# Stationary weights read with a step of two words: two blocks of 128 columns interleaved in memory, in an fp32 encoder on one core

## The chip, the core and the metric

One NeuronCore of a Trainium2 chip runs the whole kernel in one launch. The metric is device time in microseconds, the median of three timed runs. The engines are named as the profile names them: PE (TensorE, matmuls), PEld (TensorE's weight loads, which overlap PE), DVE (VectorE), ACT (ScalarE), POOL (GpSimd) and SP (SyncE, which issues the weight transfers). A matmul has a *stationary* operand, which a weight load (LDWEIGHTS) puts into the array first, and a *moving* operand, which is streamed through it column by column.

## The reference, cut to what matters

Two encoder layers over 272 tokens (16 meta tokens and 256) of width 2048, everything in float32. Layer 0 mixes tokens by a Fourier transform, layer 1 by a bidirectional state-space mixer (SSD); each is followed by a SwiGLU block of hidden width 5632.

```python
def fourier_mixer(u, w_out):
    ug = u.astype(jnp.float32).reshape(b, L, FNET_GROUPS, d // FNET_GROUPS)
    f = jnp.fft.fftn(ug, axes=(1, 3), norm="ortho").real.reshape(b, L, d)
    return f.astype(u.dtype) @ w_out
...
def bidir_ssd_mixer(u, w_in, conv_w, conv_b, dt_bias, a_log, d_skip, norm_w, w_out):
    proj = u @ w_in
...
    return gated_group_rms_norm(y, z, norm_w) @ w_out

def swiglu_ffn(u, w_gate, w_up, w_down):
    return (jax.nn.silu(u @ w_gate) * (u @ w_up)) @ w_down
```

The time goes into the products with the weight matrices: `fnet_w_out`, `ssd_w_in`, `ssd_w_out`, and two each of `ffn_w_gate`, `ffn_w_up` and `ffn_w_down`.

## The kernel before

The residual stands feature-major: 16 blocks of 128 features on the partitions, 272 (later 256) tokens along the free dimension. To keep float32 accuracy every product is made of three matmuls on operands of type float32r. `mm3` (lines 104 to 106) multiplies high part by high part, high by low and low by high; each of the three loads its stationary operand anew.

A weight matrix comes in units of 1 MiB. The host lays each matrix out in blocks (`blocks`), so that a partition's 1024 consecutive words (`RUN`) are four rows of 256 columns or two rows of 512 columns. `weights` (line 84) issues one transfer per unit on SP's queue and splits the unit in two (or more) tiles: ACT writes the high part `wh` (line 97), DVE the low part `wl` (line 98).

In most products the weights are stationary and the tokens move. `wsl` (line 108) cuts the stationary operand out of a split tile: row block k, and 128 neighbouring columns from `c0`. That is 128 consecutive words of each partition, 512 bytes. Two blocks of columns, j = 0 and 1, are worked on in turn and go to two PSUM tiles. The users are `gemm_in` (the products with `ffn_w_gate`, `ffn_w_up` and the x, B, C columns of `ssd_w_in`; moving operand `gh`, `gl`), the product with `fnet_w_out` (moving `fh`, `fl`), `down0` (the first `ffn_w_down`; moving `hh`, `hl`), `out_group` (`ssd_w_out`; moving `yh`, `yl`) and the step sizes (`w_dt`, one block of 128 columns). The moving operand is 272, 258 or 256 tokens wide.

In two products the tokens are stationary and 512 columns of weights move: the z columns of `ssd_w_in` (stationary `gh`, `gl`) and the second `ffn_w_down` in `down1` (stationary `hh`, `hl`).

The order of the work is that of the program text, but for the splits, which are given a higher priority, and the rest of the SSD mixer, which is emitted at a distance behind the large products (`later`, `slot_done`). That rest holds plain float32 matmuls (lines 605 to 665) and transposes (lines 551 to 553; 794 in the last SwiGLU).

Of the kernel before, what the change touches and what calls it, by code (L numbers as in the profile page):

```python
# [12 lines left out]
F32R = mybir.dt.float32r  # L13
# [8 lines left out]
NB = D // P            # 16 feature blocks  # L22
NM = 16                # meta tokens
KM = 64 + NM           # rows that hold them three times, from 0, 32 and 64
S = 256
L = NM + S             # 272
FG = 8                 # fnet groups
FD = D // FG           # 256
NK = L // 2 + 1        # 137 token frequencies
# [4 lines left out]
HG = H // G            # heads per group  # L34
NST = 128
DFF = 5632
NF = DFF // P          # 44
EPS = 1e-6
CA = (NM, NM + P)      # token chunk A
CB = (NM + P, L)       # token chunk B  # L40
XC, BC, CC = 0, DI, DI + G * NST      # columns of x, B, C
NRAW, NSP = 3, 4       # buffers: weights as they come (8 KiB a partition), their parts (4 + 4 KiB)
RUN = 1024             # words of a weight block that a partition holds one after the other
HC = 8                 # feature blocks of a piece of the SwiGLU hidden layer
# [4 lines left out]
def encoder(ctx: ExitStack, tc: tile.TileContext, I, out):  # L49
# [34 lines left out]
    def weights(src, k0, nk, c0, ncol):  # L84
        """Unit of a weight matrix (see blocks), rows (k0..k0+nk)*128, columns c0..c0+ncol, as (high, low) parts."""
        w = wpool.tile([P, nk, ncol], F32, tag="w", name="w", bufs=NRAW)
        k1 = RUN // ncol
        nc.sync.dma_start(w.rearrange("p (u k) c -> p u (k c)", k=k1),
                          src[k0 // k1 : (k0 + nk) // k1, c0 // ncol].rearrange("u p x -> p u x"))
        parts = []  # L90
        n = min(nk, RUN // ncol)
        for k in range(0, nk, n):
            ks = slice(k, k + n)
            wh = wpool.tile([P, n, ncol], F32R, tag="wh", name="wh", bufs=NSP)
            wl = wpool.tile([P, n, ncol], F32R, tag="wl", name="wl", bufs=NSP)
            with tc.high_priority(offset=70):
                SC.copy(wh, w[:, ks, :])  # L97
                V.tensor_tensor(out=wl, in0=w[:, ks, :], in1=wh.bitcast(F32), op=ALU.subtract)  # L98
            parts.append((wh, wl))
        return parts  # L100

    def mm3(ps, lhs, rhs, start, stop):
        """ps (+)= lhs.T @ rhs of operands split as (high, low)."""
        PE.matmul(ps, lhs[0], rhs[0], start=start, stop=False)  # L104
        PE.matmul(ps, lhs[0], rhs[1], start=False, stop=False)  # L105
        PE.matmul(ps, lhs[1], rhs[0], start=False, stop=stop)  # L106
# [4 lines left out]

    def gsl(k, a, b=L):
        return gh[:, k, a:b], gl[:, k, a:b]

    def gemm_in(src, c0, lo):
        """Two blocks of 128 columns of norm(h) @ src, feature-major, over the tokens lo.. ."""
        n = L - lo
        pss = [mmtile(), mmtile()]
        for k0 in (0, 8):
            u = weights(src, k0, 8, c0, 256)  # L120
            for k in range(8):
                for j in range(2):
                    mm3(pss[j][:, :n], wsl(u, k, j * P), gsl(k0 + k, lo), k0 + k == 0, k0 + k == NB - 1)
        return pss

    def rsqrt(pool, x, n, tag):
        """1/sqrt(x) of [P, n]: bit-level seed and three Newton steps."""
# [14 lines left out]
    def norm_block(b, wcol, lo):  # L142
        """Block b of the residual is final: operand of the next product and sum of squares."""
# [10 lines left out]
    def norm_scale(lo):  # L154
        """rbc = 1/rms of every token, the same on all partitions."""
# [19 lines left out]
    # =====================================================================  # L175
    # Fourier mixer
    # =====================================================================
    with ExitStack() as fx:
# [15 lines left out]
        # parts of x where the spectrum comes later  # L194
# [49 lines left out]
        def table(c, r):  # L244
            """Token table of chunk c scaled by 1/rms."""
            SC.activation(th[:, c, :], tok[:, c, :], AF.Identity, bias=0.0, scale=r)
            V.scalar_tensor_tensor(out=tl[:, c, :], in0=tok[:, c, :], scalar=r, in1=th[:, c, :].bitcast(F32),
                                   op0=ALU.mult, op1=ALU.subtract)

        with tc.manual_schedule():  # L250
            # residual, feature-major, parts of x, mean squares of the tokens
# [37 lines left out]
            # meta tokens: three products of parts in one, rows 0.. high high, 32.. high low, 64.. low high  # L289
# [8 lines left out]
            # token transform: cosines 0..NK-1, sines 1..NK-2  # L298
# [20 lines left out]
        # feature transform; operands in F32R have an even number of columns, so one more than is used  # L319
# [24 lines left out]
        for mp in range(NB // 2):  # L344
            pss = [mmtile(), mmtile()]
            for k0 in (0, 8):
                u = weights(I["fnet_w_out"], k0, 8, mp * 256, 256)
                for k in range(8):
                    for j in range(2):
                        mm3(pss[j][:, :L], wsl(u, k, j * P), (fh[:, k0 + k, :], fl[:, k0 + k, :]),  # L350
                            k0 + k == 0, k0 + k == NB - 1)
# [5 lines left out]
    # =====================================================================  # L357
    # SwiGLU, the hidden layer in pieces of HC feature blocks
    # =====================================================================
# [32 lines left out]
    with ExitStack() as fx:  # L392
        tmp = fx.enter_context(tc.tile_pool(name="ffn0", bufs=1))

        def down0(f0, nf, hh, hl):
            for mp in range(NB // 2):
                pss = [mmtile(), mmtile()]
                u = weights(I["w_down0"], f0, nf, mp * 256, 256)
                for k in range(nf):
                    for j in range(2):  # L400
                        mm3(pss[j][:, :L], wsl(u, k, j * P), (hh[:, k, :], hl[:, k, :]), k == 0, k == nf - 1)
# [8 lines left out]
    # =====================================================================  # L410
    # bidirectional SSD mixer
    # =====================================================================
    with ExitStack() as fx:
# [22 lines left out]
        # The products with the large weights are emitted in slots; the rest of a group follows its slots at a  # L436
        # distance, so that the tensor engine has a product to go on with meanwhile.
# [12 lines left out]
        def step_sizes():  # L450
# [6 lines left out]
            # 1/rms of the tokens of chunks A and B, one token a partition  # L457
# [14 lines left out]
            # softplus(v) = max(v, 0) + log1p(exp(-|v|)), log1p(t) = 2 atanh(t / (2 + t))  # L472
# [16 lines left out]
            # prefix sums within the chunks: inclusive forward, exclusive backward  # L489
# [42 lines left out]
        def conv(ps, blk, lo, dst):  # L532
            """Depthwise conv over the tokens lo.. of the 128 channels of block blk, then silu."""
# [14 lines left out]
        def to_tokens(src, dst, dstM):  # L548
            """[128 channels, 272 tokens] -> [tokens, 128 channels] of the chunks A, B and of the meta tokens."""
# [7 lines left out]
        def out_group(gi, q, yh, yl):  # L557
            """Residual += y @ w_out over the channels of group gi, columns 512q.. ."""
            u = weights(w_out, gi * 4, 4, q * 512, 512)
            for jp in range(2):  # L560
                pss = [mmtile(), mmtile()]
                for k in range(4):
                    for j in range(2):
                        mm3(pss[j][:, :S], wsl(u, k, (2 * jp + j) * P), (yh[:, k, :], yl[:, k, :]), k == 0, k == 3)
# [6 lines left out]
        def group_rest(gi, cT, btok, btokM, xt, xtM, zs, cb):  # L571
            """All of a group after its products with w_in."""
# [5 lines left out]
            def kernels(c):  # L578
                """Within chunk c: sum over both directions of exp(decay) dt B.C, [source, head, target]."""
# [11 lines left out]
            # weighted inputs  # L591
# [27 lines left out]
            def mix(c):  # L619
                """y of chunk c: other chunks' parts, this chunk's part, skip connection; then the gate."""  # L620
# [31 lines left out]
            def norm():  # L652
                """Grouped norm, back to feature-major."""
# [32 lines left out]
        def decays(gi):  # L686
            """Cumulated log decays of a group's heads on all partitions."""
# [7 lines left out]
        def drop(gi):  # L695
            """The half that a direction doesn't see decays to nothing."""
# [11 lines left out]
        for gi in range(G):  # L708
            if gi % 2 == 0:
# [14 lines left out]
            # x of the group  # L724
# [4 lines left out]
            def source_target(gj=gi % 2, cb=cb, bT=bT, cT=cT):  # L729
                """B.C of all sources and targets within the chunks."""  # L730
# [16 lines left out]
            # silu(z) of the group  # L747
# [27 lines left out]
    # =====================================================================  # L775
    # last SwiGLU, final norm
    # =====================================================================
    with ExitStack() as fx:
# [8 lines left out]
        def down1(f0, nf, hh, hl):  # L787
            if f0 == 0:
                # residual, one token a partition
# [59 lines left out]
def tables():  # L849
    """Constants that follow from the shapes."""  # L850
# [19 lines left out]

def blocks(w, ncol):
    """[.., rows, columns] in blocks [rows of blocks, columns of blocks, 128, (k c)]: RUN words, that is RUN / ncol
    rows 128 apart of ncol columns, one after the other."""
# [6 lines left out]
def arrays_of(inputs):  # L880
    """The matrices in blocks, the per-feature vectors one after the other in rows of 128, the tables."""
# [3 lines left out]
    a["fnet_w_out"] = blocks(inputs["fnet_w_out"][0], 256)  # L885
    a["w_z"] = blocks(w[:, :DI], 512)
    a["w_xbc"] = blocks(w[:, DI : -2 * H], 256)
    a["w_dt"] = blocks(w[:, -2 * H :], P)
    a["ssd_w_out"] = blocks(inputs["ssd_w_out"][0], 512)
    a["ffn_w_gate"] = blocks(inputs["ffn_w_gate"], 256)  # L890
    a["ffn_w_up"] = blocks(inputs["ffn_w_up"], 256)
    a["w_down0"] = blocks(inputs["ffn_w_down"][0], 256)
# [17 lines left out]
```

## Time and profile before

| what | us |
|---|---|
| timed runs, median (lowest to highest) of 3 | 2456.85 (2456.33 to 2457.35) |
| profiled execution, from first to last instruction (span) | 2455.8 |
| PE busy in it | 2428.0 (99%) |
| PEld busy | 2316.9 (94%) |
| DVE busy | 1484.5 (60%) |
| ACT busy | 1214.1 (49%) |
| POOL busy | 406.6 (17%) |

How to read it: a matmul in a stream is shown from its start until its results have drained, so consecutive matmuls overlap in the table of instructions; what one costs is the distance from its start to the start of the next. The same holds for weight loads. The span of the profiled execution lies 1.05 us under the median of the timed runs; that is what lies around the span.

### The profile page before, as it was taken

What the parts mean: (1) busy time and instruction counts of PE and PEld (TensorE: products, weight loads), DVE (VectorE), ACT (ScalarE), POOL (GpSimd) and SP (SyncE); (2) the same over time, 40 slices, a digit from 0 to 9 for tenths busy, and PEclk for the clock granted to TensorE, in tenths of its full rate; (3) what the DMA queues carried; (4) which work ended last, traced back from release to release, by engine and by line L of the source; (5) the groups of instructions that cost most, each with busy time, mean ns of one, the idle gap of its engine ahead of it and who ended that gap; (6) DMA issues with size and microseconds to landing.
All of it is one profiled execution on the core that took longest, in us unless ns stands there. A gap on an engine that the chain in (4) does not pass through costs nothing.

```text
span 2455.8 us, 42928 instructions
## 1 busy us (share of the span) xinstructions
PE 2428.0 (99%) x17958; PEld 2316.9 (94%) x17958; DVE 1484.5 (60%) x2020; ACT 1214.1 (49%) x1784; POOL 406.6 (17%) x361
## 2 busy tenths in 40 slices
PE   8999999999999999999999999999999999999998
PEld 8999999999999999888989989989999998989887
DVE  7564545545454568778668668668554555555556
ACT  6444333343434346878557558445444343444434
POOL 3111111010101112232221221112211010102000
PEclk9999999999999999999999999999999999999999
DMA  5555555555555555655455555454555555555553
GB/s 164 175 178 179 173 173 176 181 175 172 175 181 177 172 173 175 213 175 186 164 179 193 177 172 184 159 172 157 201 187 178 189 189 189 189 190 188 189 192 134
DMA packets 115506, 438.66 MB, mean 179 GB/s; under 512 B 7360, under 2 KB 8080, under 8 KB 115136
## 3 DMA queue, kind: packets, MB, share of 16 engines
q1 hardware_dynamic: 110336, 417.86, 50.4%
q0 software_dynamic: 4832, 17.99, 2.3%
q8 instruction: 141, 2.31, 0.4%
q14 instruction: 53, 0.43, 0.0%
q10 hardware_dynamic: 144, 0.07, 0.0%
HBM read 433.66 MB, written 2.23 MB: 177 GB/s over the span
## 4 chain that ended last, share of the span: by engine, by line
PE 89%; DVE 3%; DMA 3%; issue 2%; ACT 2%; POOL 1%; SPq 0%; DVEq 0%; ACTq 0%; POOLq 0%
PE mm L105 29%; PE mm L106 28%; PE mm L104 28%; DMA pb<-scr 2%; DVE wl L98 1%; PE tp L642 1%; ACT wh L97 1%; DVE ca L544 1%; PE tp L626 0%; PE tp L665 0%; DMA w<-fnet_w_out 0%; POOL pb L701 0%; ACT pb L584 0%; DMA x<-x 0%; PE tp L608 0%
## 5 line engine op out<-in xcount | busy, mean ns | idle before, releaser
L98 DVE TENSOR_TENSOR wl<-w,wh 128x1024 fp32r<-128x1024 f32 x786 | 970.0, 1236 | 840.7 <-ACT wh L97 832.7
L97 ACT CAST wh<-w 128x1024 fp32r<-128x1024 f32 x786 | 822.8, 1048 | 1096.6 <-PE mm L105 809.2
L105 PE MATMUL mm<-gl,wh 128*128 128x272 f32 (+2 forms) x3600 | 1026.0, 285 | 0.0
L106 PE MATMUL mm<-gh,wl 128*128 128x272 f32 (+2 forms) x3600 | 1022.3, 284 | 0.5 <-DVE wl L98 0.5
L104 PE MATMUL mm<-gh,wh 128*128 128x272 f32 (+2 forms) x3600 | 1022.4, 284 | 0.1
L104 PEld LDWEIGHTS mm<-gh,wh 128*128 128x128 f32 x3600 | 678.2, 188 | 1.1 <-issue 0.5
L106 PEld LDWEIGHTS mm<-gh,wl 128*128 128x128 f32 x3600 | 676.3, 188 | 0.9 <-DVE wl L98 0.7
L105 PEld LDWEIGHTS mm<-gl,wh 128*128 128x128 f32 x3600 | 676.1, 188 | 0.8 <-issue 0.5
L378 POOL TENSOR_TENSOR s<-s,rbc 128x272 f32<-128x272 f32 (+1 forms) x88 | 96.4, 1113 | 816.4 <-ACT s L377 816.4
L105 PE MATMUL mm<-hl,wh 128*128 128x272 f32 x704 | 203.7, 289 | 0.0
L106 PE MATMUL mm<-hh,wl 128*128 128x272 f32 x704 | 202.7, 288 | 0.0
L104 PE MATMUL mm<-hh,wh 128*128 128x272 f32 x704 | 200.9, 285 | 0.0
L385 POOL TENSOR_TENSOR hl<-t,hh 128x272 fp32r<-128x272 f32 (+1 forms) x88 | 97.0, 1121 | 397.1 <-ACT hh L384 397.1
L104 PE MATMUL mm<-yh,wh 128*128 128x256 f32 x512 | 146.5, 288 | 3.8 <-DVE hT L567 3.3
L105 PE MATMUL mm<-yl,wh 128*128 128x256 f32 x512 | 143.6, 281 | 0.5 <-DVE yl L671 0.5
L106 PE MATMUL mm<-yh,wl 128*128 128x256 f32 x512 | 143.5, 281 | 0.0
L105 PE MATMUL mm<-wl,hh 128*128 128x512 f32 x352 | 137.1, 390 | 0.0
L104 PE MATMUL mm<-wh,hh 128*128 128x512 f32 x352 | 137.0, 389 | 0.0
L106 PE MATMUL mm<-wh,hl 128*128 128x512 f32 x352 | 137.0, 389 | 0.0
L104 PEld LDWEIGHTS mm<-hh,wh 128*128 128x128 f32 x704 | 132.9, 189 | 0.0
L106 PEld LDWEIGHTS mm<-hh,wl 128*128 128x128 f32 x704 | 132.3, 188 | 0.0
L105 PEld LDWEIGHTS mm<-hl,wh 128*128 128x128 f32 x704 | 132.1, 188 | 0.0
(279 smaller groups left out, 2858.5 us busy)
## 6 DMA issues: line engine op xcount, KB each, us to landing
w<-ffn_w_gate SPq DMA_DIRECT2D x88, 1024.0 KB, 5.1
w<-ffn_w_up SPq DMA_DIRECT2D x88, 1024.0 KB, 5.1
w<-w_down SPq DMA_DIRECT2D x80, 1024.0 KB, 5.1
w<-w_xbc SPq DMA_DIRECT2D x48, 1024.0 KB, 5.2
w<-w_z SPq DMA_DIRECT2D x32, 1024.0 KB, 5.3
w<-ssd_w_out SPq DMA_DIRECT2D x32, 1024.0 KB, 5.1
w<-fnet_w_out SPq DMA_DIRECT2D x16, 1024.0 KB, 5.1
pb<-scr POOLq DMA_DIRECT2D x32, 512.0 KB, 5.6
```

The source lines that it names most:

```text
L97: SC.copy(wh, w[:, ks, :])
L98: V.tensor_tensor(out=wl, in0=w[:, ks, :], in1=wh.bitcast(F32), op=ALU.subtract)
L104: PE.matmul(ps, lhs[0], rhs[0], start=start, stop=False)
L105: PE.matmul(ps, lhs[0], rhs[1], start=False, stop=False)
L106: PE.matmul(ps, lhs[1], rhs[0], start=False, stop=stop)
L378: GP.tensor_tensor(out=s1, in0=s1, in1=rbc[:, lo:], op=ALU.mult)
L385: GP.tensor_tensor(out=hl[:, f, :], in0=t2, in1=hh[:, f, :].bitcast(F32), op=ALU.subtract)
L544: V.scalar_tensor_tensor(out=a[:, o0:o1], in0=u[:, i0 : i0 + o1 - o0], scalar=w(j), in1=a[:, o0:o1], op0=ALU.mult, op1=ALU.add)
L642: PE.matmul(py[:, e * HD : (e + 1) * HD], kern[c][:, e, :], xt[:, c, e * HD : (e + 1) * HD], start=True, stop=True)
```

## The change

The host lays the columns of each pair of 128-column blocks out in turn (`paired`): column 0 of the first block, column 0 of the second, column 1 of the first, and so on. It does so for every matrix whose weights are the stationary operand, apart from `w_dt`, which has one block. `ssl` then cuts a block out of a split tile with a step of two words: 128 words out of 256 consecutive ones, 1024 bytes, from word 0 for the first block of the pair and from word 1 for the second. Transfers and splits keep their shapes and sizes, each matmul gets the same numbers in the same places of the array, and the order of the instructions is the same on every engine; of the 17,696 matmuls of the program 15,168 have a stationary operand with step 2 in place of step 1, and nothing else differs. (The rest of the diff takes comments out.)

```diff
+    def ssl(u, k, j):
+        each = u[0][0].shape[1]
+        return tuple(x.rearrange("p k (m c i) -> p k m i c", c=P, i=2)[:, k % each, j // 2, j % 2, :]
+                     for x in u[k // each])
...
     def gemm_in(src, c0, lo):
...
-                    mm3(pss[j][:, :n], wsl(u, k, j * P), gsl(k0 + k, lo), k0 + k == 0, k0 + k == NB - 1)
+                    mm3(pss[j][:, :n], ssl(u, k, j), gsl(k0 + k, lo), k0 + k == 0, k0 + k == NB - 1)
...
-                        mm3(pss[j][:, :L], wsl(u, k, j * P), (fh[:, k0 + k, :], fl[:, k0 + k, :]),
+                        mm3(pss[j][:, :L], ssl(u, k, j), (fh[:, k0 + k, :], fl[:, k0 + k, :]),
...
-                        mm3(pss[j][:, :L], wsl(u, k, j * P), (hh[:, k, :], hl[:, k, :]), k == 0, k == nf - 1)
+                        mm3(pss[j][:, :L], ssl(u, k, j), (hh[:, k, :], hl[:, k, :]), k == 0, k == nf - 1)
...
-                        mm3(pss[j][:, :S], wsl(u, k, (2 * jp + j) * P), (yh[:, k, :], yl[:, k, :]), k == 0, k == 3)
+                        mm3(pss[j][:, :S], ssl(u, k, 2 * jp + j), (yh[:, k, :], yl[:, k, :]), k == 0, k == 3)
...
+def paired(w):
+    m = w.reshape(*w.shape[:-1], w.shape[-1] // (2 * P), 2, P)
+    return np.swapaxes(m, -1, -2).reshape(w.shape)
...
-    a["fnet_w_out"] = blocks(inputs["fnet_w_out"][0], 256)
+    a["fnet_w_out"] = blocks(paired(inputs["fnet_w_out"][0]), 256)
...
-    a["w_xbc"] = blocks(w[:, DI : -2 * H], 256)
+    a["w_xbc"] = blocks(paired(w[:, DI : -2 * H]), 256)
...
-    a["ssd_w_out"] = blocks(inputs["ssd_w_out"][0], 512)
-    a["ffn_w_gate"] = blocks(inputs["ffn_w_gate"], 256)
-    a["ffn_w_up"] = blocks(inputs["ffn_w_up"], 256)
-    a["w_down0"] = blocks(inputs["ffn_w_down"][0], 256)
+    a["ssd_w_out"] = blocks(paired(inputs["ssd_w_out"][0]), 512)
+    a["ffn_w_gate"] = blocks(paired(inputs["ffn_w_gate"]), 256)
+    a["ffn_w_up"] = blocks(paired(inputs["ffn_w_up"]), 256)
+    a["w_down0"] = blocks(paired(inputs["ffn_w_down"][0]), 256)
```

## Rows read from the trace of the kernel before

**Rows 1.** The page: busy time, slices of the clock, and the chain that ended last.

```profile
span 2455.8 us, 42928 instructions
...
PE 2428.0 (99%) x17958; PEld 2316.9 (94%) x17958; DVE 1484.5 (60%) x2020; ACT 1214.1 (49%) x1784; POOL 406.6 (17%) x361
...
PEclk9999999999999999999999999999999999999999
...
PE 89%; DVE 3%; DMA 3%; issue 2%; ACT 2%; POOL 1%; SPq 0%; DVEq 0%; ACTq 0%; POOLq 0%
```

**Rows 2.** The page's groups of matmuls with stationary weights: line, tiles, count.

```profile
L104 PE MATMUL mm<-gh,wh 128*128 128x272 f32 (+2 forms) x3600 | 1022.4, 284 | 0.1
...
L104 PE MATMUL mm<-hh,wh 128*128 128x272 f32 x704 | 200.9, 285 | 0.0
...
L104 PE MATMUL mm<-yh,wh 128*128 128x256 f32 x512 | 146.5, 288 | 3.8 <-DVE hT L567 3.3
```

**Rows 3.** The same by shape: matmuls on gh and fh.

```profile
L104 PE MATMUL mm<-gh,wh 128*128 128x272 f32 x2064 | 591.2, 287 | 0.0
L104 PE MATMUL mm<-gh,wh 128*128 128x256 f32 x1408 | 394.5, 280 | 0.1
...
L104 PE MATMUL mm<-fh,wh 128*128 128x272 f32 x256 | 73.1, 286 | 0.0
...
L104 PE MATMUL mm<-gh,wh 128*128 128x258 f32 x128 | 36.6, 286 | 0.0
```

**Rows 4.** Windows of one shape each: stretch, length, busy time and instructions, clock, DMA.

```profile
160.00:940.00 780.00, 780.00 (x6242) 780.00 (x6241) 405.91 (x466) 315.87 (x383) 112.47 (x104) 1.00 0.53 176
1720.00:1885.00 165.00, 165.00 (x1413) 165.00 (x1412) 86.75 (x101) 71.33 (x89) 32.57 (x30) 1.00 0.56 190
1162.50:1173.40 10.90, 10.90 (x94) 10.90 (x94) 8.21 (x16) 9.61 (x20) 6.07 (x5) 1.00 0.47 165
953.80:965.00 11.20, 11.20 (x96) 11.20 (x95) 11.06 (x26) 6.99 (x9) 0.00 (x0) 1.00 0.39 137
1137.90:1159.30 21.40, 21.40 (x94) 17.39 (x93) 17.10 (x22) 18.90 (x31) 0.91 (x1) 1.00 0.55 194
2025.00:2065.00 40.00, 40.00 (x178) 33.12 (x177) 21.97 (x21) 15.46 (x17) 2.18 (x2) 1.00 0.54 185
```

**Rows 5.** Weight loads around a stop of the tensor engine: start, duration, instruction.

```profile
1441.25 0.19 PEld L104 LDWEIGHTS mm<-yh,wh 128*128 128x128 f32 x1 [1.84 <-DVE hT L567]
1441.36 0.19 PEld L105 LDWEIGHTS mm<-yl,wh 128*128 128x128 f32 x1
1441.48 0.19 PEld L106 LDWEIGHTS mm<-yh,wl 128*128 128x128 f32 x1
1442.10 0.19 PEld L104 LDWEIGHTS mm<-yh,wh 128*128 128x128 f32 x1 [0.43 <-DVE hT L567]
```

**Rows 6.** The matmuls of the same stretch, by line, with the duration in ns.

```profile
L104 PE MATMUL mm<-yh,wh 128*128 128x256 f32 x1 | 0.4, 386 | 1.6 <-DVE hT L567 1.6
L105 PE MATMUL mm<-yl,wh 128*128 128x256 f32 x1 | 0.3, 280 | 0.0
L106 PE MATMUL mm<-yh,wl 128*128 128x256 f32 x1 | 0.3, 276 | 0.0
```

**Rows 7.** Timeline of plain float32 matmuls with 64 moving columns: their loads.

```profile
1204.38 1.75 PEld L642 LDWEIGHTS tp<-xt,pb 128*128 128x128 f32 x15 [0.24 <-issue]
```

**Rows 8.** Loads by line: of a split product, of a transpose.

```profile
L104 PEld LDWEIGHTS mm<-hh,wh 128*128 128x128 f32 x704 | 132.9, 189 | 0.0
...
L794 PEld LDWEIGHTS tp<-ident,hT 128*128 128x128 f32 x32 | 3.4, 141 | 0.6 <-ACT htok L795 0.4
```

**Rows 9.** Matmuls at 1107.9 us by line; the load behind the last comes 0.27 us later.

```profile
L106 PE MATMUL mm<-gh,wl 128*128 128x272 f32 x1 | 0.3, 288 | 0.0
L105 PE MATMUL mm<-gl,wh 128*128 128x272 f32 x1 | 0.3, 287 | 0.0
L104 PE MATMUL mm<-gh,wh 128*128 128x272 f32 x1 | 0.3, 285 | 0.0
```

**Rows 10.** Timeline of that stretch: start, duration, matmul and loads.

```profile
1107.79 0.19 PEld L104 LDWEIGHTS mm<-gh,wh 128*128 128x128 f32 x1
...
1107.90 0.28 PE L104 MATMUL mm<-gh,wh 128*128 128x272 f32 x1
...
1108.17 0.19 PEld L665 LDWEIGHTS tp<-dg,yg 128*128 128x128 f32 x1 [0.20 <-ACT btokM L555]
```

## The prediction

> **What bounds the kernel now.** First the page: PE is busy 99% of the span and holds 89% of the chain that ended last, at a granted clock of 9 tenths or more in every slice, which is the 2.4 GHz level; DVE stands at 60% and ACT at 49% [rows 1]. So the distance between matmul starts sets the time. The change touches nothing but how the stationary operand of many of these matmuls is read, so the next question is how many, and the one after it is whether a load has anything to do with that distance.
>
> How many: the matmuls of line 104 on `gh`, `hh`, `yh` [rows 2] and, by shape, on `gh` and `fh` [rows 3]. At 272 columns 2064 + 704 + 256 = 3024, less the 16 of the step sizes, which keep their layout: 3008. At 256 columns 1408 on `gh` and 512 on `yh`, at 258 columns 128. With lines 105 and 106 that is three times as many: 9024, 4224, 1536 and 384, together 15,168 loads.
>
> What one costs: the windows of a single shape [rows 4], each length over its matmuls, less two that had begun before the window. At 272 columns 780.0 us / 6240 = 125.0 ns; at 256 on `gh` 165.0 / 1411 = 116.9; at 256 on `yh` 10.9 / 92 = 118.5; at 258 11.2 / 94 = 119.1. The sum is 1128 + 494 + 182 + 46 = 1850 us, three quarters of the span. The clock is 1.00 in all four, and at 2.4 GHz 272 columns alone take 113.3 ns, 256 take 106.7: some 10 to 12 ns are added to each.
>
> What a load costs: in a stream it starts together with the matmul ahead of its own and is out of sight. It comes into sight where PE has stopped. At 1441.25 us a load starts after a wait, and the next load starts at 1441.36 [rows 5]; the matmul between shows 386 ns in place of 280 [rows 6]. So a load that hides behind nothing costs 386 - 280 = 106 ns. In a row of plain float32 matmuls of only 64 moving columns, 15 loads take 1.75 us; less the 0.19 of the last that is 1.56 / 14 = 111 ns from load to load [rows 7]. Load time is thus 106 to 111 ns, and the matmul that hides it lasts 125.0, 116.9, 118.5 or 119.1. The cover is there everywhere, but thin: 14, 6, 7 and 8 ns over the 111.
>
> **The change part by part.**
>
> *Transfers, splits, order.* Shapes, bytes and order of the instructions are those of before; ACT and DVE write and read the same tiles. Cost 0, covered by nothing because nothing is added.
>
> *The read of the load.* It brings the same 128 words from 1024 bytes in place of 512. No row shows a stationary operand with a step, so the cost is bounded. From below: nothing, since what is read word by word is as much as before. From above: a read that goes by bytes passed, not by words taken, takes twice as long, 111 + 106 = 217 ns, and sets the distance itself: 9024 x 92.0 + 4224 x 100.1 + 1536 x 98.5 + 384 x 97.9 = 830 + 423 + 151 + 38 = 1442 us. Between these ends I go by the transposes of line 794: their loads, also of 128 x 128 float32, show 141 ns against the 188 to 189 of the others [rows 8], 48 ns less; so these 512 bytes are read in about 106 - 48 = 58 ns, and 1024 bytes at that pace in 116 ns. The read of this port can pass over 1024 bytes in about the time that a load has now. I take 0 for the read. If it did take the full 116, it would still be under every distance, if by 1 ns at 256 columns. The price when the cover is gone: from 116.9 ns up each further ns costs 4.2 us, from 118.5 on 5.8, from 125 on 15.2.
>
> Here a rule of the Trainium skill can be set beside that. SBUF — State Buffer, Specifications (TRN2), says that SBUF works in lines of 16 bytes, that a line wants at least two hits for full bandwidth, and that each cross to a new line costs something. With a step of two words there are exactly two hits in a line, so by the first half the load keeps its time and the sum is 0 as well; by the second half it crosses 64 lines in place of 32, which speaks against the change and belongs to the second rival below. No row here shows either.
>
> *The read of the moving operand.* Could the load slow or speed the matmul under which it runs? At 1107.90 us a matmul of 272 columns runs with no load beside it, since the next load starts at 1108.17 [rows 10]; it shows 285 ns, the two ahead of it, each with a load beside, 288 and 287 [rows 9], and the mean of its group is 287 [rows 3]. At 256 columns the last one before the second stop shows 276 against 280 [rows 6]. So a load beside it costs a matmul 2 to 4 ns at most, and the greater part of the 10 to 12 ns belongs to the moving operand alone. Cost of the change here: between a gain of those 2 to 4 ns and a loss; I take 0.
>
> *Sum.* 2455.8 + 0 for the profiled execution, with 1.05 us around it the median of now: 2457 us.
>
> **The rivals.**
>
> *Slower by half and more: the load becomes the bound.* The 1442 us above, so 3899 us. For it: the cover is thin, and no strided load is in the trace. Against it: line 794's loads. Chance 0.11.
>
> *Slower by some per cent: a longer load, or one that disturbs the stream.* This decides as soon as a load takes over 118 ns, 7 more than now (4.9 us at 4.2 us per ns, and that is 0.2%). At a tenth more, 122 ns: 4224 x 5.1 + 1536 x 3.5 + 384 x 2.9 = 28 us, 2485 us. At a fifth more, 133 ns, it would be 9024 x 8 + 4224 x 16.1 + 1536 x 14.5 + 384 x 13.9 = 168 us, 2625 us. For disturbance: which addresses the load reads is not without effect. Where 512 columns of weights move, a matmul takes 40.0 / 176 = 227 ns over stationary `hh`, whose blocks all start alike, and 21.4 / 92 = 233 over stationary `gh`, whose blocks are 1088 bytes apart [rows 4]. At those 6 ns on each of 15,168 matmuls it would be 91 us, 2548 us. Against it: the 2 to 4 ns above. Chance 0.19, most of it below 2560.
>
> *Faster: part of the added 10 to 12 ns goes.* If the load and the moving operand now hinder each other (the load takes a word in the time in which the stream takes two), a load that passes over memory at the same pace as the stream could do so less. The bound is the stream alone at 272 columns and the load's 111 ns at the others: 9024 x 11.7 + 4224 x 5.9 + 1536 x 7.5 + 384 x 8.1 = 106 + 25 + 12 + 3 = 146 us, 2311 us; by the 2 to 4 ns that rows 6 and 9 leave to the load it is 30 to 60 us, 2397 to 2427. For it: 227 against 233 ns. Against it: the matmuls without a load beside them are hardly shorter. Chance 0.25, four fifths of it above 2390.
>
> The Trainium skill, TensorE: Matmul & The Clock Gate, Step-by-step: what each phase is for, has two separate read ports, one for the moving operand and one for the load, so that loading takes nothing from a running matmul. By that rule neither the disturbance nor the gain exists and the sum stays 0; 285 against 287 ns agrees with it nearly, 227 against 233 does not.
>
> **How the numbers follow.** No change 0.45, faster 0.25, slower 0.30 (0.19 by some per cent, 0.11 by half). Within 0.2%, 4.9 us, is about what a measurement of this kernel can tell from no change; that is only 0.32 ns on each of the 15,168 matmuls, which is why the middle case does not get more. The predicted time is that of the likeliest, 2457 us; by itself it would be 2452 to 2462. The range reaches to 2390 (four fifths of the faster case) and to 2560 (nearly all of the slower one without the doubled load): 0.45 + 0.20 + 0.16 is some 0.8.
>
> **What would show it.** Right: windows of one shape in the changed kernel again at 125.0, 116.9, 118.5 and 119.1 ns, and at a stop of PE again some 106 ns from a load to the next. A load that has become longer shows there first, and in its duration of 188 ns. If the stream is disturbed or freed, the load's duration stays and the distance of the matmuls changes at 272 columns as well as at 256; if the load is the bound, all shapes come to the same distance. Windows over stationary `gh` and `hh`, which the change leaves alone, must stay at 233 and 227. The forecast fails if reading every other word is not free for the load, or if the 10 to 12 ns are the load's doing after all.

## The result and the profile after

The changed kernel is slower by 0.9%: 2479.18 us (median; 2476.81 to 2480.64) against 2457.10 of the kernel before. The ratio is 1.0087, with a 95% interval of 1.0073 to 1.0102. Its profiled execution spans 2477.9 us, 22.1 more than before [rows 1]. That is inside the stated range and on the side of the second rival; the likeliest case, no change, did not come.

First the page of the kernel after, for the engines, the matmuls that were counted and their loads:

```profile
span 2477.9 us, 42928 instructions
...
PE 2449.5 (99%) x17958; PEld 2339.2 (94%) x17958; DVE 1484.1 (60%) x2020; ACT 1213.7 (49%) x1784; POOL 406.8 (16%) x361
...
L104 PEld LDWEIGHTS mm<-gh,wh 128*128 128x128 f32 x3600 | 703.3, 195 | 1.0 <-issue 0.4
...
L104 PEld LDWEIGHTS mm<-hh,wh 128*128 128x128 f32 x704 | 137.5, 195 | 0.0
```

DVE, ACT and POOL are busy for the same time to half a microsecond; PE has 21.5 us more. The loads over `hh` show 195 ns in place of 189 [rows 8]. Next the windows of one shape each, in the order and columns of [rows 4]: 272 columns, 256 on `gh`, 256 on `yh`, 258, then the two products that were left alone, over stationary `gh` and over stationary `hh`.

```profile
160.00:940.00 780.00, 780.00 (x6201) 780.00 (x6200) 402.56 (x460) 311.67 (x376) 110.42 (x102) 1.00 0.52 175
1730.00:1895.00 165.00, 165.00 (x1377) 165.00 (x1377) 85.34 (x97) 69.11 (x88) 32.42 (x30) 1.00 0.55 185
1167.80:1178.80 11.00, 11.00 (x94) 11.00 (x94) 8.32 (x16) 9.60 (x20) 6.09 (x5) 1.00 0.45 150
958.30:969.50 11.20, 11.20 (x95) 11.20 (x94) 11.05 (x26) 7.09 (x9) 0.00 (x0) 1.00 0.39 136
1143.30:1164.60 21.30, 21.30 (x94) 17.29 (x93) 16.56 (x22) 18.90 (x30) 0.91 (x1) 1.00 0.54 194
2042.00:2082.00 40.00, 40.00 (x178) 33.13 (x177) 21.42 (x21) 15.48 (x16) 1.98 (x2) 1.00 0.56 184
```

Less two matmuls a window as before, the distances are 780 / 6199 = 125.8 ns (125.0 before), 165 / 1375 = 120.0 (116.9), 11 / 92 = 119.6 (118.5) and 11.2 / 93 = 120.4 (119.1). All kinds of about 256 columns have come to the same 120 ns, whatever they were; a matmul of 272 columns has become 0.8 ns longer. Where the tokens are stationary it is 21.3 / 92 = 231.5 over `gh` and 40 / 176 = 227.3 over `hh`, as before (232.6 and 227.3; one matmul more or less in the shorter window is 2.5 ns). The sum is 9024 x 0.8 + 4224 x 3.1 + 1536 x 1.1 + 384 x 1.3 = 7.2 + 13.1 + 1.7 + 0.5 = 22.5 us, against 22.1 in the span: nothing is missing, and the 256 columns hold two thirds of it.

Last the load by itself, at stops of the tensor engine, as in [rows 5] (start, duration, instruction), and the matmul between, by line, with its ns:

```profile
1447.63 0.19 PEld L104 LDWEIGHTS mm<-yh,wh 128*128 128x128 f32 x1 [1.69 <-DVE hT L573]
1447.75 0.20 PEld L105 LDWEIGHTS mm<-yl,wh 128*128 128x128 f32 x1
1447.87 0.20 PEld L106 LDWEIGHTS mm<-yh,wl 128*128 128x128 f32 x1
1448.48 0.20 PEld L104 LDWEIGHTS mm<-yh,wh 128*128 128x128 f32 x1 [0.41 <-DVE hT L573]
```

```profile
L104 PE MATMUL mm<-yh,wh 128*128 128x256 f32 x1 | 0.4, 394 | 1.5 <-DVE hT L573 1.5
...
L105 PE MATMUL mm<-yl,wh 128*128 128x256 f32 x1 | 0.3, 281 | 0.0
```

The next load starts 0.12 us behind the first where it was 0.11, and the matmul that waits for its own load shows 394 ns in place of 386 [rows 6]. So a load with nothing beside it takes 394 - 281 = 113 ns by the one reading, 7 more than before, and some 120 by the other, which goes in steps of 10 ns.

### The profile page after: what moved, and what is told of

It reads as the page before. It is cut to its first block, busy times and chain, and to the rows that moved or that the text cites. A ratio compares the mean times of both kernels' runs of the same rounds, so it can differ in the third digit from the quotient of the medians.

```text
span 2477.9 us, 42928 instructions
## 1 busy us (share of the span) xinstructions
PE 2449.5 (99%) x17958; PEld 2339.2 (94%) x17958; DVE 1484.1 (60%) x2020; ACT 1213.7 (49%) x1784; POOL 406.8 (16%) x361
## 4 chain that ended last, share of the span: by engine, by line
PE 92%; DVE 3%; ACT 2%; DMA 1%; issue 1%; POOL 0%; SPq 0%; DVEq 0%; ACTq 0%; POOLq 0%
PE mm L104 29%; PE mm L105 29%; PE mm L106 29%; DVE wl L98 1%; PE tp L648 1%; ACT wh L97 1%; DMA pb<-scr 1%; DVE ca L550 1%; ACT pb L590 0%; PE tp L632 0%; DMA w<-fnet_w_out 0%; PE tp L671 0%; PE tp L614 0%; PE tp L611 0%; DMA x<-x 0%
## 5 line engine op out<-in xcount | busy, mean ns | idle before, releaser
L104 PEld LDWEIGHTS mm<-gh,wh 128*128 128x128 f32 x3600 | 703.3, 195 | 1.0 <-issue 0.4
L106 PEld LDWEIGHTS mm<-gh,wl 128*128 128x128 f32 x3600 | 703.3, 195 | 0.7 <-DVE wl L98 0.5
L105 PEld LDWEIGHTS mm<-gl,wh 128*128 128x128 f32 x3600 | 703.2, 195 | 0.7 <-issue 0.5
```

## The experiments

**Two theories.** A load is covered by the matmul under which it runs. Theory A: the load itself has become longer, and where its cover was thin it now sets the distance of the matmuls. Theory B: the load still takes its time out of sight, but its wider read disturbs the moving stream under which it runs, at every width.

**One part alone.** Step 2 only where 272 columns move (`e1_only272`), and only where 256 or 258 do (`e2_only256`); the host pairs the columns of those matrices alone.

```diff
-                    mm3(pss[j][:, :n], ssl(u, k, j), gsl(k0 + k, lo), k0 + k == 0, k0 + k == NB - 1)
+                    mm3(pss[j][:, :n], ssl(u, k, j) if lo == 0 else wsl(u, k, j * P), gsl(k0 + k, lo), k0 + k == 0, k0 + k == NB - 1)
```

That is `gemm_in` in the first of them, against the changed kernel; `out_group` goes back to `wsl` there. In the second the condition is `lo > 0`, and the product with `fnet_w_out` and `down0` go back to `wsl`.

> Step 2 only in the 9024 loads under 272 moving columns; the 6144 under 256 and 258 columns are contiguous again. Theory A (the load itself has become 8 ns longer and sets the distance where its cover was thin): nearly nothing is left, since 125 ns still cover a load of 117; what the windows of the changed kernel show at 272 columns, 0.7 ns x 9024 = 6 us, so 2463 us; 256 columns back at 117 to 118.5 ns. Theory B (the doubled read disturbs the moving stream, whatever its width, 22 us / 15,168 = 1.45 ns each): 9024 x 1.45 = 13 us, 2470 us.

> The other part: step 2 only in the 6144 loads under 256 and 258 columns. Theory A: 4224 x 3.0 + 1536 x 1.7 + 384 x 1.2 = 16 us, 2473 us, and both kinds of 256 columns at the same 120.0 ns, since the load sets them. Theory B: 6144 x 1.45 = 9 us, 2466 us.

Measured: 2463.97 us for 272 alone (ratio 1.0028, 1.0017 to 1.0040) and 2473.50 for 256 and 258 alone (1.0068, 1.0055 to 1.0080): 6.8 and 16.3 us over the 2457.16 of before. The second is what A forecast (16, where B had 9); the first is A's 6 and not B's 13, but A took those 6 from the windows of the changed kernel and did not explain them. The two parts add up to 23 us, against 22 for the whole. The windows at 272 and at 256 columns, first of e1, then of e2:

```profile
160.00:940.00 780.00, 780.00 (x6206) 780.00 (x6205) 403.11 (x462) 311.76 (x376) 110.51 (x102) 1.00 0.51 175
1725.00:1885.00 160.00, 160.00 (x1371) 160.00 (x1370) 84.61 (x96) 69.24 (x87) 32.57 (x30) 1.00 0.55 190
```

```profile
160.00:940.00 780.00, 780.00 (x6242) 780.00 (x6241) 405.93 (x465) 315.88 (x383) 112.50 (x104) 1.00 0.51 176
1725.00:1890.00 165.00, 165.00 (x1377) 165.00 (x1377) 84.80 (x96) 69.71 (x88) 32.38 (x30) 1.00 0.54 185
```

In e1 the distances are 780 / 6204 = 125.7 and 160 / 1369 = 116.9, in e2 780 / 6240 = 125.0 and 165 / 1375 = 120.0. Each part costs what it costs in the whole change.

**A narrower stream.** If the load sets the distance at 256 columns, fewer columns gain nothing. In the last SwiGLU's gate and up products 224 columns move in place of 256 in 15 of 16 row blocks, so 32 tokens are left out of those sums; once with step 1 (`e5_w224`), once in the changed kernel (`e6_w224_step2`, shown here; the first has `wsl(u, k, j * P)` in place of `ssl(u, k, j)`).

```diff
-                    mm3(pss[j][:, :n], ssl(u, k, j), gsl(k0 + k, lo), k0 + k == 0, k0 + k == NB - 1)
+                    m = 224 if lo == NM and k0 + k else n
+                    mm3(pss[j][:, :m], ssl(u, k, j), gsl(k0 + k, lo, lo + m), k0 + k == 0, k0 + k == NB - 1)
```

> The kernel before (step 1), but the last SwiGLU's gate and up products move 224 columns in place of 256 in 15 of 16 row blocks (32 tokens are left out of those sums): 3960 matmuls. Theory A (distance = the longer of stream and load): the stream would need 93.3 + 10.2 = 103.5 ns, the load with its 111.5 ns from load to load is longer, so 111.5 ns and 3960 x 5.4 = 21 us less, 2436 us. Theory B (the load only disturbs the stream): 103.5 ns, 3960 x 13.4 = 53 us less, 2404 us.

> The same cut to 224 moving columns, in the changed kernel (step 2). Theory A: the load sets the distance at 256 columns already, so it stays at 120 ns and so does the time, 2479 us. Theory B: stream of 103.5 ns plus the same 3 ns as at 256 columns, 3960 x 13.4 = 53 us less, 2426 us.

Measured: 2437.13 us with step 1 (ratio 0.9921, 0.9906 to 0.9936), 2474.60 with step 2 (1.0074, 1.0058 to 1.0091). A window of these products in each, step 1 and step 2:

```profile
1720.00:1850.00 130.00, 130.00 (x1164) 130.00 (x1163) 72.69 (x83) 59.18 (x75) 27.88 (x26) 1.00 0.58 196
```

```profile
1740.00:1870.00 130.00, 130.00 (x1094) 130.00 (x1093) 65.38 (x69) 54.90 (x68) 25.61 (x23) 1.00 0.56 190
```

With step 1 it is 130 / 1162 = 111.9 ns: the load's own pace of 111 [rows 7], not the 103.5 that the expectation estimates for the stream. With step 2 it is 130 / 1092 = 119.0, and 32 columns fewer, by that estimate 13 ns of stream, have bought 1 ns against the changed kernel. A holds at these widths, B alone does not: the load's pace from load to load has gone from 111.9 to 119 or 120 ns. Where the last nanosecond between 224 and 256 columns comes from is not shown.

**More steps.** What does a read with a step cost? Step 4 (four blocks of 128 in turn), step 8 (all eight blocks of a split tile in turn) and step 3 (which takes other words than the product wants), in the same 15,168 loads.

```diff
-        each = u[0][0].shape[1]
-        return tuple(x.rearrange("p k (m c i) -> p k m i c", c=P, i=2)[:, k % each, j // 2, j % 2, :]
+        each, ncol = u[0][0].shape[1:]
+        b = k % each * (ncol // P) + j
+        return tuple(x.rearrange("p k c -> p (k c)").rearrange("p (g c i r) -> p g i c r", g=2, i=4, r=1)[:, b // 4, b % 4]
                     for x in u[k // each])
```

That is `ssl` with step 4; the host lays the eight blocks of 128 columns of a split tile out to match (`in_turn`). Step 8 has `g=1, i=8` and `b // 8, b % 8`. Step 3 takes every third word from a start of its own for each block.

> Step 4 in place of 2: four blocks of 128 in turn, a load reads 128 words out of 2048 bytes, one word in each 16 bytes. Theory A with a price for each 16 bytes touched (32 more cost 8 ns, so 96 more cost 24): load 132.5, distance 136 at every width, 9024 x 11 + 4224 x 19.1 + 1536 x 17.6 + 384 x 16.5 = 213 us, 2670 us. If the 8 ns are a fixed price of any step, 2479 us. If a read with only one word taken of each 16 bytes goes at half speed (the skill's two hits in a line), load about 217 ns, some 3900 us.

> Step 3: a load reads 128 words out of 1536 bytes (other words than the product wants), 96 pieces of 16 bytes, of which a third give two words and two thirds one. If the time goes by pieces of 16 bytes once there are more than 64 of them (step 4: 128 pieces, 217 ns, 1.7 ns each): load 163 ns, distance 166 to 179 (step 4 had 16 ns over its load, step 2 had 3.5), 3130 to 3320 us. If one word alone in its 16 bytes anywhere halves the whole load: 4134 us as with step 4. If the price were smooth in the step: between 2479 and 2700 us.

> Step 8: 128 words out of 4096 bytes, one word in every second piece of 16 bytes. If the pieces touched count (128, as with step 4): 4134 us, load 329 ns in the table, distance 233. If the bytes passed count: the load takes about twice as long again, 434 ns, distance 450, some 7400 us.

Measured: step 3 3261.48 us (ratio 1.3276, 1.3256 to 1.3296), step 4 4134.11 us (1.6826, 1.6803 to 1.6849), step 8 4257.36 us (a single run). The loads of line 104 on `gh` (busy time, ns of one), of step 3, step 4 and step 8:

```profile
L104 PEld LDWEIGHTS mm<-gh,wh 128*128 128x128 f32 x3600 | 945.5, 263 | 0.8 <-issue 0.5
```

```profile
L104 PEld LDWEIGHTS mm<-gh,wh 128*128 128x128 f32 x3600 | 1183.4, 329 | 0.8 <-ACT st L612 0.2 <-issue 0.2
```

```profile
L104 PEld LDWEIGHTS mm<-gh,wh 128*128 128x128 f32 x3600 | 1214.1, 337 | 0.8 <-issue 0.2 <-ACT st L612 0.2
```

And a window of the products with 272 columns in each, in the same order:

```profile
160.00:1200.00 1040.00, 1040.00 (x5914) 1039.96 (x5914) 381.97 (x427) 291.27 (x344) 101.32 (x92) 1.00 0.36 125
```

```profile
160.00:1500.00 1340.00, 1340.00 (x5745) 1339.96 (x5745) 369.67 (x411) 283.63 (x336) 98.95 (x91) 1.00 0.27 95
```

```profile
160.00:1500.00 1340.00, 1340.00 (x5550) 1339.96 (x5551) 360.10 (x403) 275.85 (x328) 95.96 (x88) 1.00 0.26 91
```

| step | bytes passed | pieces of 16 bytes | load shown, ns | distance, ns |
|---|---|---|---|---|
| 1 | 512 | 32 | 188 to 189 | 111.9 where the load sets it |
| 2 | 1024 | 64 | 195 | 120.0 |
| 3 | 1536 | 96 | 263 | 1040 / 5912 = 175.9 |
| 4 | 2048 | 128 | 329 | 1340 / 5743 = 233.3 |
| 8 | 4096 | 128 | 337 | 1340 / 5548 = 241.5 |

From step 2 to 3 and from 3 to 4 there are 32 more pieces of 16 bytes each, and 55.9 and 57.4 ns more: 1.75 and 1.79 ns a piece. Step 8 passes twice the bytes of step 4 and touches as many pieces; it costs 8 ns more, not twice as much. So the pieces touched count, and not the bytes passed. From step 1 to 2 the 32 more pieces cost only 8 ns. At 1.77 ns 64 pieces need 113 ns, just over the 106 that 128 neighbouring words took [rows 6]; by this reading step 2 is the place where the price by pieces overtakes the price by words. For step 4 the flat extrapolation that stood in its expectation (24 ns) was wrong and the half speed right, to 6% of the time. The Trainium skill (SBUF — State Buffer, Specifications (TRN2)) has lines of 16 bytes, wants two hits in a line for full bandwidth and names a penalty for each new line. These runs agree in kind, but two hits in a line still cost 8 ns on 112 here.

**Does a load that is out of sight disturb the stream?** Two runs change only loads under 512 moving columns, where 227 to 233 ns cover them. First step 2 in the tokens that are stationary there, so that these products take other tokens (`e3_tokens_step2`); then, after its result, step 1 with another start (`e9_start64`).

```diff
-                    mm3(pz[c], gsl(k, a, b), wsl(u, k % 4, 0, 512), k == 0, k == NB - 1)
+                    mm3(pz[c], tuple(g[:, k, NM + c : L : 2] for g in (gh, gl)), wsl(u, k % 4, 0, 512), k == 0, k == NB - 1)
...
-                    mm3(pd, (hh[:, k, ts], hl[:, k, ts]), wsl(us[k // 4], k % 4, 0, 512), k == 0, k == nf - 1)
+                    mm3(pd, (hh[:, k, c : S : 2], hl[:, k, c : S : 2]), wsl(us[k // 4], k % 4, 0, 512), k == 0, k == nf - 1)
```

And the other start, in the second (`NM` is 16, so 64 bytes into a row for the first half of the tokens and 448 for the second):

```diff
-                ts = slice(c * P, (c + 1) * P)
+                ts = slice((c * 6 + 1) * NM, (c * 6 + 9) * NM)
```

> The kernel before, but the stationary tokens of the z product and of the last SwiGLU's second product are read with step 2 (tokens of one parity in place of a chunk of 128, so these two products take other tokens); 1824 loads, each under 512 moving columns. Theory A: the loads show 195 ns in place of 188, and the time stays, 2457 us, because 227 ns cover a load of 117. Theory B: the stream is disturbed there too, 1824 x 1.5 to 3 ns = 3 to 5 us, 2460 to 2462 us.

> The kernel before (step 1 everywhere), but in the last SwiGLU's second product the stationary tokens start 64 bytes (first half) or 448 bytes (second half) into each row in place of 0 or 512 (other tokens than the product wants); 1056 loads under 512 moving columns, each still of 512 consecutive bytes. It asks what the loads of the third run did to the stream that covered them (226.9 to 233.3 ns). If where a load reads matters to the stream whatever its step: 230 to 233 ns, as over the tokens of the z product, 3 to 7 us more, 2460 to 2464 us. If only the step matters: 226.9 ns, 2457 us.

Measured: e3 2463.69 us (ratio 1.0029, 1.0017 to 1.0040), e9 2462.36 us (1.0021, 1.0012 to 1.0030). A window over stationary `hh`, of e3, then of e9:

```profile
2030.00:2065.00 35.00, 35.00 (x152) 28.95 (x151) 18.81 (x19) 13.53 (x13) 0.00 (x0) 1.00 0.53 187
```

```profile
2027.00:2065.00 38.00, 38.00 (x166) 30.72 (x165) 20.75 (x20) 13.75 (x14) 0.00 (x0) 1.00 0.53 191
```

And the loads of it by line, of e3, then of e9:

```profile
L104 PEld LDWEIGHTS mm<-wh,hh 128*128 128x128 f32 x352 | 68.0, 193 | 13.9
```

```profile
L104 PEld LDWEIGHTS mm<-wh,hh 128*128 128x128 f32 x352 | 66.2, 188 | 14.9
```

The distance is 35 / 150 = 233.3 ns in e3 and 38 / 164 = 231.7 in e9, where it was 227.3. Theory A by itself said that nothing would happen in e3, and fell there: 1056 x 6.0 = 6.3 us came from loads that have 100 ns of cover. And e9 shows that no step is needed for it: loads of 512 consecutive bytes and 188 ns do nearly the same when they start 64 or 448 bytes into a row. Nor does a step always cost: over `gh`, which stood near 233 before, 21.4 us of e3 (1137.5 to 1158.9 us) hold 94 matmuls, as many as before [rows 4]. So where a load reads matters to the stream under it, at a price of 4 to 6 ns here, and the 227 ns over `hh` before was the favourable case. How the places interact is not settled by these runs.

**The rest at 272 columns.** Is the 0.8 ns there thin cover, or this disturbance? With 304 columns moved in place of 272 in 5760 matmuls (the 32 more go to columns that are not used) the cover is 138 ns wide; once with step 1 (`e10_w304`, which has `wsl`), once with step 2 (`e11_w304_step2`, shown here).

```diff
+                    a, m = (k0 + k) * L + lo, 304 if lo == 0 and k0 + k < NB - 1 else n
+                    mm3(pss[j][:, :m], ssl(u, k, j), tuple(g.rearrange("p b t -> p (b t)")[:, a : a + m] for g in (gh, gl)),
+                        k0 + k == 0, k0 + k == NB - 1)
```

> The kernel before (step 1) with a wider cover: where the gate, up, B and x products move 272 columns, 304 are moved in 15 of 16 row blocks (the 32 more run on into the next block's tokens and go to columns that are not used; the 272 are as before): 5760 matmuls. Distance there 304 / 2.4 + 11.7 = 138.4 ns. It is the base line for the next run.

> The same in the changed kernel (step 2). What is left of the change at 272 columns, 0.8 ns, is either the thin cover (125 over a load of 120 from load to load) or a disturbance of the stream by the place from which the load reads. If the cover: under 138 ns it is gone, the window shows the distance of the run before to 0.1 ns. If the disturbance: 0.8 ns or more stay, as the 5 to 6 ns did under 512 columns.

A single run each: 2548.26 us with step 1, 2564.02 with step 2. The same stretch of the first gate and up products, step 1, then step 2:

```profile
165.00:220.00 55.00, 55.00 (x401) 55.00 (x400) 23.86 (x25) 20.39 (x25) 9.92 (x10) 1.00 0.48 164
```

```profile
165.00:220.00 55.00, 55.00 (x398) 55.00 (x398) 23.10 (x26) 20.65 (x26) 10.38 (x10) 1.00 0.47 158
```

55 / 399 = 137.8 and 55 / 396 = 138.9 ns. The difference of about 1 ns stays with 18 ns of cover to spare, so by these windows the rest at 272 columns is the disturbance and not the cover. It is no fixed price either: over `hh`, where 272 columns move in both, 80 us of the changed kernel (850 to 930) hold 638 matmuls, 80 / 636 = 125.8 ns, and 80 us of e11 (905 to 985) hold 641, 80 / 639 = 125.2, with the same loads. Why it differs is not shown. The two total times, 15.8 us apart where the whole change costs 22, are single runs and are not used for this. Each of the two theories holds in its own place.

## Why the prediction was right, and where it was wrong

The range held because it was drawn wide enough to take in the second rival, with a chance of 0.19; the point of 2457 us rests on a read that costs nothing, and that did not hold.

*What bounds the kernel.* Right: the distance of the matmuls is the whole story. Four distances times four counts give 22.5 us of the 22.1, and every other engine is as it was.

*Transfers, splits, order: 0.* Right; DVE and ACT are busy for the same time within 0.5 us.

*The read of the load: "I take 0 for the read."* This is the step that failed. The row behind it led near the measured time: 512 bytes in about 58 ns, so 1024 in 116, and the load at stops now takes 113 to 120. The price by pieces bears it out, for 58 ns over 32 pieces of 16 bytes are 1.8 ns a piece, beside the 1.75 and 1.79 measured; a pace by bytes, as I put it, would have doubled again from step 4 to step 8. But I called that "in about the time that a load has now" and took 0, and the sentence behind it, that the full 116 "would still be under every distance, if by 1 ns at 256 columns", set the load's bare time against the distance of matmuls. From load to load there are some 5 ns more than that: my own [rows 7] had 111 beside 106. 116 + 5 is 121, over 116.9, 118.5 and 119.1, and 120.0 was measured. At 120 ns the price list of the prediction, 4.2 us per ns from 116.9 and 5.8 from 118.5 on, gives 4224 x 3.1 + 1536 x 1.5 + 384 x 0.9 = 16 us, which is what e2 measured.

*The read of the moving operand: 0.* Mis-sized: 0.8 ns at 272 columns, 7 us. There it lies below the bound of 2 to 4 ns that the prediction took from single matmuls, but that bound does not hold everywhere: under 512 columns e3 and e9 measured 6.0 and 4.4. The two distances at 512 columns that differed before, 227 over `hh` and 233 over `gh`, did mean what the rival took them for; e3 and e9 move the one nearly to the other.

*The rivals.* The slower case by some per cent is the one that came, at its small end, by both of its mechanisms: the load past 118 ns for 16 us and the disturbance for 7. Its turning point, a load of over 118 ns, was right only if load time means from load to load. The doubled load did not come with step 2; e4 shows that it comes with step 4, and at 4134 us. The gain did not come: no shape got shorter, and in e5, with a narrower stream, it is the load's pace that stands in the way.

*The signs.* The windows named as signs showed a mixture that they had not been given for: the load's duration grew (188 to 195) and the shapes of 256 and 258 columns met at one distance, as for a load that is the bound, while 272 columns stayed apart from them at 125.8 and grew too, as for a stream that is disturbed. `gh` and `hh` stayed, as they had to.

No run beats the kernel before on the whole product; the one that is faster, e5, leaves 32 tokens out.

## What to carry to other kernels

A stationary operand may be read with a step of two 4-byte words at a small price (8 ns a load here), but not with a larger one: from load to load three words took 176 ns and four took 233, where one word took 112. Before calling an operation hidden, compare like with like: the cover of a load is the distance of the matmuls less the distance from load to load, taken from a stretch in which loads follow each other, not less the bare duration of a load. Cover of 6 to 8 ns on 100 is no cover for an edit whose price is only known to 10%.

## What was not expected of the hardware

Where a load reads from is felt by the stream that hides it, though the load has time to spare: 227.3 ns against 231.7 and 233.3 at 512 columns with the same number of words, and about 1 ns at 138. The Trainium skill (TensorE: Matmul & The Clock Gate, Step-by-step: what each phase is for) has separate read ports for the two, so that a load takes nothing from a running matmul. In these runs the stream is not fully independent of where its load reads, and what they share is not shown. And a step of 8 words, which touches as many pieces of 16 bytes as a step of 4, still takes 241.5 in place of 233.3 ns, in a single run.
